# The down-projection of a ConvFFN written as seven block products, with operands made entry by entry

## The chip, the cores and the metric

The kernel runs on one core of one Trainium2 chip. The metric is the device time of one launch in microseconds (us). The measurement of this kernel before the change gave a median of 1247.1 us over three runs (1246.14 to 1247.32). One further execution was recorded by the hardware profiler; its own time is 1248.44 us, and its span, from the first to the last instruction, is 1246.7 us.

The engines are called PE (TensorE matmuls), PEld (its weight loads), DVE (VectorE), ACT (ScalarE), POOL (GpSimd) and SP (SyncE, which issues most DMA transfers).

## The reference

The kernel computes one layer of a streaming encoder for a prompt of 1024 tokens and eight sample sequences of 16 tokens (1152 tokens in all). A token mixer (spatial gating beside latent attention) is followed by a layer norm and a gated feed-forward network with a depthwise convolution of width 3:

```
up   = h @ w_up                       # (tokens, 1024) x (1024, 2*2816)
c    = causal_conv3(up) + b           # per channel, over the tokens
act  = silu(c[:, :2816]) * c[:, 2816:]
y    = act @ w_down                   # (tokens, 2816) x (2816, 1024)
out  = layer_norm(alpha * h + y)
```

The change concerns `act @ w_down` and what lies just ahead of it. Inputs and outputs are float32.

## The kernel before, in words

**Precision.** A float32 product is made of three matmuls on rounded parts. `split` writes the rounded value hi with ACT (`L60`) and the rest lo = x - hi with DVE (`L61`); `mm3` multiplies hi by hi, hi by lo and lo by hi (`L72` to `L74`), all summed in the same PSUM bank.

**Tiles.** There are 9 tiles of 128 tokens (8 of the prompt, one of the sample rows) and 22 blocks of 128 channels (`NF`). PSUM has eight banks of 512 columns, in four pools called A (3 banks), B (2), C (1) and D (2).

**Up-projection.** One iteration for each of the 22 channel blocks. Each makes seven block products (`product_mm`, `L932` to `L934`) instead of eight; ACT copies and DVE additions (`product`, `L1031` and `L1033`) put them into the output tiles `U`. An addition out of a bank frees it for the next product. The list `after(i)` is worked off between the products of the next iteration: the convolution (`conv`, ACT `L1038`, DVE `L1039` and `L1040`) and silu of one half, the convolution of the other half, and `gate` (DVE `L1052`), whose product of 1168 columns POOL writes to DRAM as `ad[i]` (`L1053`). The weights of the next iteration are added and split meanwhile (`L904`, `L907` and others, then `L60` and `L61`).

**Down-projection.** `load_down(i)` reads the activations of channel block i back from DRAM and its 128 x 1024 weights, and splits both into two tiles of a ring of 16. Blocks 0 to 3 are loaded during the last up-projection iteration. The 22 blocks are taken in five groups (`BLK`: 4, 4, 4, 4, 6). For each group, each token tile and each half of the 1024 output columns, `down_mm` sums the group's products in one PSUM bank, and DVE adds the bank to `y` in SBUF (`L1154`, `L1156`, in the last group `L1170` and `L1172`). So a block, once loaded, serves nine token tiles and two halves. In the first group `y` is first loaded and multiplied and shifted by the first layer norm's gain and bias (`L1148`, `L1149`). The last group is followed, tile by tile, by the second layer norm and the output. Its last token tile (the sample rows) computes its second half in two pieces of 256 columns, and the norm of that tile is what runs after the last matmul.

**Order.** A scheduler sets the order on each engine within the dependences; `pin` (`keep_in_program_order`) holds an instruction at the place where it is written. SP's DMA queue is worked off in order: a transfer that waits holds all that stand behind it.

## Time and profile before

| | |
|---|---|
| median of three runs | 1247.1 us (1246.14 to 1247.32) |
| profiled execution, its own time | 1248.44 us |
| its span | 1246.7 us |
| busy PE, PEld | 1227.5 us (98%), 1137.6 us |
| busy DVE, ACT, POOL | 844.6 us (68%), 533.1 us (43%), 97.7 us (8%) |
| last up-projection matmul starts | 972.34 us |
| last matmul of the down-projection starts | 1238.46 us |
| mean granted TensorE clock | 0.998 |

The profile gives, for each instruction, its line, its engine, the tile written and the tiles read, and its time; for idle time it names the event that ended it. Matmuls overlap on PE: the time shown for one is longer than its distance to the next, so its price is read from start to start. DMA issues show the time from issue to landing.

### The profile page before, as it was taken

Reading aid. Unit: us, or ns where it says so; the run is one execution under the profiler, and the core shown is the slowest. Engines: PE = TensorE matmul, PEld = TensorE weight load, DVE = VectorE, ACT = ScalarE, POOL = GpSimd, SP = SyncE. Lnnn points to the kernel's source line nnn. Section 1 sums busy time; section 2 is a strip of 40 time slices with the busy share of each in tenths; the row PEclk is TensorE's granted clock in tenths of the full one; section 3 lists DMA queues with packets and bytes.
Section 4 is the critical chain, followed back from the end, with each engine's and each line's share of the span. In section 5 each row is a group of like instructions: output and inputs, shape, how many; then the busy total and the mean of one; then the engine's idle time right before and its main releaser. Section 6 shows DMA issues by size and latency. Waiting matters only on the chain.

```text
span 1246.7 us, 19600 instructions
## 1 busy us (share of the span) xinstructions
PE 1227.5 (98%) x7737; PEld 1137.6 (91%) x7737; DVE 844.6 (68%) x1642; ACT 533.1 (43%) x1098; POOL 97.7 (8%) x229
## 2 busy tenths in 40 slices
...
DMA packets 35853, 116.47 MB, mean 93 GB/s; under 512 B 5120, under 2 KB 6272, under 8 KB 35760
## 3 DMA queue, kind: packets, MB, share of 16 engines
...
q8 instruction: 61, 1.00, 0.3%
q14 instruction: 32, 0.26, 0.1%
...
## 4 chain that ended last, share of the span: by engine, by line
PE 97%; ACT 1%; DVE 1%; DMA 1%; issue 0%; SPq 0%; ACTq 0%; DVEq 0%
PE A L934 8%; PE A L933 7%; PE A L932 7%; PE A L72 7%; PE A L73 7%; PE A L74 7%; PE D L72 7%; PE D L73 7%; PE D L74 7%; PE D L934 4%; PE D L933 4%; PE D L932 4%; PE B L72 2%; PE B L73 2%; PE B L74 2%; PE B L934 2%
## 5 line engine op out<-in xcount | busy, mean ns | idle before, releaser
L932 PE MATMUL A<-b,wu 128*128 128x288 f32 x704 | 207.6, 296 | 0.5 <-DVE U L1031 0.4
L933 PE MATMUL A<-b,wu 128*128 128x288 f32 x704 | 207.9, 296 | 0.0
L934 PE MATMUL A<-b,wu 128*128 128x288 f32 x704 | 206.0, 298 | 0.0
L932 PEld LDWEIGHTS A<-b,wu 128*128 128x128 f32 x704 | 132.4, 188 | 1.0 <-DVE U L1031 0.6
L933 PEld LDWEIGHTS A<-b,wu 128*128 128x128 f32 x704 | 132.8, 189 | 0.0
L934 PEld LDWEIGHTS A<-b,wu 128*128 128x128 f32 x704 | 131.1, 188 | 0.0
L934 PE MATMUL D<-b,wu 128*128 128x288 f32 x352 | 104.8, 298 | 0.0
L932 PE MATMUL D<-b,wu 128*128 128x288 f32 x352 | 104.1, 296 | 0.0
L933 PE MATMUL D<-b,wu 128*128 128x288 f32 x352 | 104.0, 295 | 0.0
L60 ACT ACTIVATE wu<-sc 128x512 fp32r<-128x512 f32 x66 | 41.8, 633 | 138.2 <-PE A L934 105.0
L60 ACT ACTIVATE b<-cbox 128x1024 fp32r<-128x1024 f32 (+1 forms) x40 | 25.6, 676 | 142.7 <-PE B L73 42.2
L61 DVE TENSOR_TENSOR wu<-sc,wu 128x512 fp32r<-128x512 f32 x66 | 46.2, 701 | 46.5 <-ACT wu L60 45.0
L1039 DVE SCALAR_TENSOR_TENSOR cbox<-U,raw,cbox 128x1168 f32<-128x1168 f32 x44 | 63.0, 1431 | 9.4 <-ACT cbox L1038 9.3
L933 PEld LDWEIGHTS D<-b,wu 128*128 128x128 f32 x352 | 66.4, 189 | 0.1
L932 PEld LDWEIGHTS D<-b,wu 128*128 128x128 f32 x352 | 66.1, 188 | 0.3 <-ACT b L60 0.3
L934 PEld LDWEIGHTS D<-b,wu 128*128 128x128 f32 x352 | 66.1, 188 | 0.0
L1040 DVE SCALAR_TENSOR_TENSOR cbox<-U,raw,cbox 128x1168 f32<-128x1168 f32 x44 | 63.0, 1431 | 0.8
L1038 ACT ACTIVATE cbox<-U,raw 128x1168 f32<-128x1168 f32 x44 | 60.0, 1363 | 7.3 <-DVE U L1031 7.1
L60 ACT ACTIVATE wu<-raw 128x512 fp32r<-128x512 f32 x66 | 41.6, 631 | 47.5 <-PE D L934 23.6
L1033 ACT ACTIVATE U<-A 128x288 f32<-128x288 f32 (+2 forms) x154 | 53.0, 368 | 17.5 <-PE A L934 17.5
L61 DVE TENSOR_TENSOR wu<-raw,wu 128x512 fp32r<-128x512 f32 x66 | 45.0, 685 | 14.5 <-ACT wu L60 14.5
L932 PE MATMUL B<-b,wu 128*128 128x288 f32 x176 | 52.1, 296 | 1.7 <-ACT hbox L855 1.7
...
## 6 DMA issues: line engine op xcount, KB each, us to landing
raw<-in_w_up SPq DMA_DIRECT2D x44, 512.0 KB, 3.2
ad<-cbox POOLq DMA_DIRECT2D x22, 584.0 KB, 3.1
cbox<-ad SPq DMA_DIRECT2D x22, 584.0 KB, 6.1
raw<-in_w_down SPq DMA_DIRECT2D x22, 512.0 KB, 5.7
xr<-in_xT SPq DMA_DIRECT2D x14, 512.0 KB, 4.1
y<-in_x SPq DMA_DIRECT2D x9, 512.0 KB, 3.6
nd<-y SPq DMA_DIRECT2D x9, 512.0 KB, 2.6
raw<-in_w_uv_in SPq DMA_DIRECT2D x8, 512.0 KB, 4.0
```

The costliest lines, as they stand in the source:

```text
L60: act.activation(hi, src, AF.Copy)
L61: dve.tensor_tensor(lo, src, f(hi), ALU.subtract)
L72: pe.matmul(out, lh, rh, start=first, stop=False)
L73: pe.matmul(out, lh, rl, start=False, stop=False)
L74: pe.matmul(out, ll, rh, start=False, stop=last)
L932: hold(pe.matmul(o_, lh, rh, start=first and k == 0, stop=False, skip_group_check=not first))
L933: hold(pe.matmul(o_, lh, rl, start=False, stop=False, skip_group_check=not first))
L934: hold(pe.matmul(o_, ll, rh, start=False, stop=k == 3, skip_group_check=not first))
L1033: act.activation(dst, src, AF.Copy)
L1038: act.activation(v, U[:, 2:n + 2], AF.Identity, bias=cw[:, fi, 3:4], scale=cw[:, fi, 2:3])
L1039: dve.scalar_tensor_tensor(v, U[:, 1:n + 1], cw[:, fi, 1:2], v, ALU.mult, ALU.add)
L1040: dve.scalar_tensor_tensor(v, U[:, 0:n], cw[:, fi, 0:1], v, ALU.mult, ALU.add)
```

## The change

The down-projection of the prompt's 1024 tokens is written as a product of 2 x 2 blocks: the tokens in two halves of 512 (`HT`), the channels in 11 pairs of blocks (`NPF`; the even block of a pair is one half, the odd one the other), and the output columns in two halves of 512. It uses seven block products with sums of activation blocks and sums of weight blocks, where eight products had been made. The sample rows are multiplied as before, as a ninth tile called `lone`.

The sums of activations are made in `after(i)` for odd i, when both blocks of a pair are there: four DVE operations of 512 columns (`L1069`, `L1070`, `L1074`, `L1075` of the new file) in the tiles of both gates. POOL then writes `ad[i-1]`, `an` (1024 columns) and `ax` (512 columns) to DRAM (`L1071`, `L1076`, `L1077`), beside `ad[i]` (`L1059`).

The operands are made by `produce()`, in the order of `ENTRY`: phases "2", "1", "65", "73" and "4", each over the 11 pairs. An entry reads its activations and weights (SP, `L1103` to `L1105` in the first two phases), makes sums of weights with DVE, and splits into two slots (one in phase "4") of a ring of 14. Phase "65" also writes a sum of weights to DRAM (`td`), which phase "4" reads. An entry of "2" or "1" serves four token tiles and the sample rows (18 matmuls), of "65" and "73" two products (24), of "4" one (12). `fill_ring` makes entries as far ahead as the ring has room. The entries 0 to 3 are made in the last up-projection iteration, in place of blocks 0 to 3.

Each product's bank is summed over all 11 pairs, so PSUM is added into `y` (`take`) at the end of a phase only, and the eight banks hold the running sums all the time. `y` is loaded and prepared (`first_y`) during the first two phases. At the end the second layer norm of the tiles follows phase "73" and runs beside phase "4", whose last token tile is computed in two pieces of 256 columns of one bank; the norm of tile 7, now the last one, follows.

```diff
+    an = [drp.tile([P, SEQ], F32, tag=f"an{i}", name=f"an{i}") for i in range(NPF)]
+    ax = [drp.tile([P, HT], F32, tag=f"ax{i}", name=f"ax{i}") for i in range(NPF)]
+    td = [drp.tile([P, HT], F32, tag=f"td{i}", name=f"td{i}") for i in range(NPF)]
...
         def gate():
             dve.tensor_tensor(cg[:, :n], ca[:, :n], cg[:, :n], ALU.mult)
-            pool.dma_start(ad[i], cg[:, :n])
+            if i % 2:
+                pool.dma_start(ad[i], cg[:, :n])
         l.append(gate)
-        return l
+        if i % 2 == 0:
+            even[:] = [ca, cg]
+            return l
+        spare, E = even
+        a00, a10, a01, a11 = E[:, :HT], E[:, HT:SEQ], cg[:, :HT], cg[:, HT:SEQ]
+        s5, s6, s3 = ca[:, :HT], ca[:, HT:SEQ], spare[:, :HT]
+
+        def sums_a():
+            dve.tensor_tensor(s5, a10, a11, ALU.add)
+            dve.tensor_tensor(a10, a00, a10, ALU.subtract)
+            pool.dma_start(ad[i - 1], E[:, :n])
+
+        def sums_b():
+            dve.tensor_tensor(s6, s5, a00, ALU.subtract)
+            dve.tensor_tensor(s3, a01, s6, ALU.subtract)
+            pool.dma_start(an[i // 2], ca[:, :SEQ])
+            pool.dma_start(ax[i // 2], s3)
+        return l + [sums_a, sums_b]
...
+    made, wslot, gone, raws = [], [0], [0], [raw_tile]
+    ENTRY = [(ph, p) for ph in ("2", "1", "65", "73", "4") for p in range(NPF)]
+    araw = [ctile[e] for e in (0, 3, 4)]
+
+    def slot():
+        wslot[0] += 1
+        return ring[(wslot[0] - 1) % len(ring)].rearrange("p c k i -> p (c k i)")
+
+    def both(ap, m):
+        return ap[:, :2 * m].rearrange("p (c m) -> p c m", c=2)
+
+    def produce():
+        ph, p = ENTRY[len(made)]
+        k = len(made)
+        ra = araw[k] if k < 3 else ctile[k % 3]
+        wr = raws[k % len(raws)]()
+        dn, up = a["w_down"][2 * p], a["w_down"][2 * p + 1]
+        if ph in ("2", "1"):
+            f_ = 2 * p + (ph == "2")
+            pin(sp.dma_start(ra[:, :HT], ad[f_][:, :HT]))
+            pin(sp.dma_start(ra[:, HT:HT + n - SEQ], ad[f_][:, SEQ:]))
+            pin(sp.dma_start(wr, a["w_down"][f_]))
+            sa, sb = slot(), slot()
+            wd, ac, lone = both(sa, D), both(sb, HT), both(sa[:, 2 * D:], P)
+            split(wd[:, 0], wd[:, 1], wr)
+            split(ac[:, 0], ac[:, 1], ra[:, :HT])
+            l4 = lone.rearrange("p c (b s) -> p c b s", b=NB)
+            split(l4[:, 0], l4[:, 1], ra[:, HT:HT + n - SEQ].rearrange("p (b s) -> p b s", b=NB)[:, :, 2:])
+            made.append((wd, ac, lone))
+            return
+        if ph == "4":
+            pin(sp.dma_start(ra[:, :HT], ad[2 * p + 1][:, HT:SEQ]))
+            pin(sp.dma_start(wr[:, :HT], td[p]))
+            sa = slot()
+            wd, ac = both(sa, HT), both(sa[:, D:], HT)
+            split(wd[:, 0], wd[:, 1], wr[:, :HT])
+            split(ac[:, 0], ac[:, 1], ra[:, :HT])
+            made.append((wd, ac, None))
+            return
+        if ph == "65":
+            pin(sp.dma_start(wr, dn))
+            wx = raws[(k + 1) % len(raws)]() if len(raws) > 1 else raw_tile()
+            pin(sp.dma_start(wx, up))
+            pin(sp.dma_start(ra[:, :SEQ], an[p]))
+            dve.tensor_tensor(wr[:, HT:], wr[:, HT:], wr[:, :HT], ALU.subtract)
+            dve.tensor_tensor(wr[:, :HT], wx[:, HT:], wr[:, HT:], ALU.subtract)
+        else:
+            pin(sp.dma_start(wr[:, :HT], dn[:, HT:]))
+            pin(sp.dma_start(wr[:, HT:], up[:, HT:]))
+            pin(sp.dma_start(ra[:, :HT], ad[2 * p][:, HT:SEQ]))
+            pin(sp.dma_start(ra[:, HT:SEQ], ax[p]))
+            dve.tensor_tensor(wr[:, :HT], wr[:, HT:], wr[:, :HT], ALU.subtract)
+        sa, sb = slot(), slot()
+        wd, ac = both(sa, D), both(sb, D)
         split(wd[:, 0], wd[:, 1], wr)
-        split(ac[:, 0, :SEQ], ac[:, 1, :SEQ], ra[:, :SEQ])
-        acs = ac[:, :, SEQ:].rearrange("p c (b s) -> p c b s", b=NB)
-        split(acs[:, 0], acs[:, 1], ra[:, SEQ:n].rearrange("p (b s) -> p b s", b=NB)[:, :, 2:])
-        ops[i] = (ac, wd)
+        split(ac[:, 0], ac[:, 1], ra[:, :SEQ])
+        if ph == "65":
+            dve.tensor_tensor(wx[:, :HT], wx[:, :HT], wr[:, :HT], ALU.subtract)
+            pool.dma_start(td[p], wx[:, :HT])
+        made.append((wd, ac, None))
...
-                    load_down(len(ops))
+                    produce()
...
-    BLK = [range(0, 4), range(4, 8), range(8, 12), range(12, 16), range(16, NF)]
-    dn, seq_d = [0], list("DBADBADBAC")
-
-    def down_mm(t, cols, blk):
-        b = bank(seq_d[dn[0] % len(seq_d)])
-        dn[0] += 1
-        m = cols.stop - cols.start
-        tok = slice(t * P, (t + 1) * P)
-        for j in blk:
-            ac, wd = ops[j]
-            mm3(b[:, :m], ac[:, 0, tok], ac[:, 1, tok], wd[:, 0, cols], wd[:, 1, cols], j == blk[0], j == blk[-1])
-        return b[:, :m]
-
...
+    raws.append(lambda: y2.tile([P, D], F32, tag="rw", name="rw", bufs=4))
+    sums = y2.tile([P, TT, 2], F32, tag="sums", name="sums")
+    ylate = {("2", 1 + 2 * t): t for t in range(4)}
+    ylate.update({("1", 1 + 2 * e): t for e, t in enumerate((8, 4, 5, 6, 7))})
+
+    def first_y(t):
         pin(sp.dma_start(y[t], nd[t]))
+        pin(dve.tensor_tensor(y[t], y[t], lg1, ALU.mult))
+        pin(dve.tensor_tensor(y[t], y[t], lb1, ALU.add))
+
+    def dmm(out, l, lc, r, rc, first, start, stop):
+        pe.matmul(out, l[:, 0, lc], r[:, 0, rc], start=start, stop=False, skip_group_check=not first)
+        pe.matmul(out, l[:, 0, lc], r[:, 1, rc], start=False, stop=False, skip_group_check=not first)
+        pe.matmul(out, l[:, 1, lc], r[:, 0, rc], start=False, stop=stop, skip_group_check=not first)
+
...
+    def take(t, c, b, fresh, acc=None):
+        yv = y[t][:, half[c]]
+        if acc is None and not fresh:
+            pin(dve.tensor_tensor(yv, yv, b, ALU.add))
+        else:
+            kw = {} if acc is None else {"accum_out": sums[:, t, c:c + 1]}
+            pin(dve.scalar_tensor_tensor(yv, yv, ALPHA if fresh else 1.0, b, ALU.mult, ALU.add, **kw))
+
+    def fill_ring(left):
+        while len(made) < len(ENTRY):
+            need = 1 if ENTRY[len(made)][0] == "4" else 2
+            if wslot[0] - gone[0] + need > len(ring) - left:
+                break
+            produce()
+
+    seg = [slice(e * P, (e + 1) * P) for e in range(2 * NT)]
+    full, P1 = slice(0, P), NPF - 1
+    Y = [bank(g) for g in "BBDD"]
+    L = [bank("A") for _ in range(2)]
+    X = Z = None
+    for k, (ph, p) in enumerate(ENTRY[:4 * NPF]):
+        fill_ring(2)
+        if (ph, p) in ylate:
+            first_y(ylate[ph, p])
+        wd, ac, lone = made[k]
+        if ph == "2":
+            for tp in range(NT):
+                dmm(Y[tp], ac, seg[tp], wd, half[0], True, p == 0, p == P1)
+        elif ph == "1":
+            if p == 0:
+                X = [bank(g) for g in "ACBB"]
+            for tp in range(NT):
+                dmm(X[tp], ac, seg[tp], wd, half[0], True, p == 0, p == P1)
+        else:
+            if p == 0 and ph == "65":
+                Z = [bank(g) for g in "DDAA"]
+            for tp in range(NT):
+                dmm(X[tp], ac, seg[tp + (NT if ph == "65" else 0)], wd, half[0], False, False, p == P1)
+            for tp in range(NT):
+                dmm(Z[tp], ac, seg[tp + (0 if ph == "65" else NT)], wd, half[1], ph == "65", p == 0 and ph == "65", p == P1)
+        if lone is not None:
+            for c in range(2):
+                dmm(L[c], lone, full, wd, half[c], True, ph == "2" and p == 0, ph == "1" and p == P1)
+        gone[0] += 2
+        if p == P1:
+            if ph == "2":
+                for tp in range(NT):
+                    take(tp, 0, Y[tp], True)
+            elif ph == "1":
+                for tp in range(NT):
+                    take(tp, 0, X[tp], False, True)
+                for c in range(2):
+                    take(NP, c, L[c], True, True)
+            elif ph == "65":
+                for tp in range(NT):
+                    take(tp, 1, X[tp], True)
+                for tp in range(NT):
+                    take(tp + NT, 1, Z[tp], True)
+            else:
+                for tp in range(NT):
+                    take(tp + NT, 1, X[tp], False, True)
+                for tp in range(NT):
+                    take(tp, 1, Z[tp], False, True)
+    fill_ring(0)
+    fin = made[4 * NPF:]
...
+    def end_mm(tp, cols):
+        for p, (wd, ac, _) in enumerate(fin):
+            dmm(X[tp][:, cols], ac, seg[tp], wd, cols, False, False, p == P1)
...
+    for tp, l in enumerate(((8, 0, 1), (2, 4), (3, 5), (6,))):
+        if tp < 3:
+            end_mm(tp, half[0])
+        else:
+            end_mm(tp, quart[0])
+            end_mm(tp, quart[1])
+        for e in l:
+            if e == 6:
+                for q in (2, 3):
+                    pin(dve.bn_stats(s6[:, q], yt[:, quart[q]]))
+            cur = norm_a(e, zs[zi % 3])
+            zi += 1
+            norm_b(prev)
+            prev = cur
+        if tp < 3:
+            take(tp + NT, 0, X[tp], True, True)
...
+    for e in (0, 1):
+        yv = yt[:, quart[e]]
+        pin(dve.scalar_tensor_tensor(yv, yv, ALPHA, X[3][:, quart[e]], ALU.mult, ALU.add))
+        pin(dve.bn_stats(s6[:, e], yv))
...
```

**DVE in an odd iteration of the up-projection.** The rows follow the last convolution. `U` is an output tile of the up-projection, `cbox` the storage of the gates, `wu`, `sc` and `raw` belong to the next weights. Before:

```order
L1031 TENSOR_TENSOR U<-U,B 128x288
L61 TENSOR_TENSOR wu<-raw,wu 128x512
L1052 TENSOR_TENSOR cbox<-cbox 128x1168
L61 TENSOR_TENSOR wu<-raw,wu 128x512
L61 TENSOR_TENSOR wu<-sc,wu 128x512
L907 TENSOR_TENSOR sc<-sc,raw 128x512
L1031 TENSOR_TENSOR U<-U,D 128x288
```

Now:

```order
L1035 TENSOR_TENSOR U<-U,B 128x288
L61 TENSOR_TENSOR wu<-raw,wu 128x512
L1057 TENSOR_TENSOR cbox<-cbox 128x1168
L61 TENSOR_TENSOR wu<-raw,wu 128x512
L1069 TENSOR_TENSOR cbox<-cbox 128x512
L1070 TENSOR_TENSOR cbox<-cbox 128x512
L1074 TENSOR_TENSOR cbox<-cbox 128x512
L61 TENSOR_TENSOR wu<-sc,wu 128x512
L1075 TENSOR_TENSOR cbox<-cbox 128x512
L911 TENSOR_TENSOR sc<-sc,raw 128x512
L1035 TENSOR_TENSOR U<-U,D 128x288
```

The four sums stand between the gate and the addition out of bank D.

**SP between the up- and the down-projection.** `ad_44..` are the activations in DRAM, `cbox` the raw activations in SBUF, `nd` the saved residual. Before, around blocks 2 to 4:

```order
L1066 DMA cbox<-ad_4456 128x1168
L1134 DMA raw<-in_ln_b 128x1024
L1139 DMA y_10742<-nd_4444 128x1024
L1139 DMA y_10743<-nd_4445 128x1024
L1147 DMA y_10744<-nd_4446 128x1024
L1066 DMA cbox<-ad_4457 128x1168
L1068 DMA raw<-in_w_down 128x1024
```

Now, entries 3, 4 and the start of 5:

```order
L1103 DMA cbox<-ad_4460 128x512
L1104 DMA cbox<-ad_4460 128x144
L1105 DMA raw<-in_w_down 128x1024
L1189 DMA raw<-in_ln_b 128x1024
L1272 DMA raw<-in_ln_g 128x1024
L1103 DMA cbox<-ad_4462 128x512
L1104 DMA cbox<-ad_4462 128x144
L1105 DMA raw<-in_w_down 128x1024
L1103 DMA cbox<-ad_4464 128x512
```

The read of `ad_4462` is entry 4's. Its target is the tile from which the last `ax` is written; it and all behind it stand after that write.

**PE at the end of phase "1".** The first entries of phase "65" follow; the bank letters are pools, `b_...` ring slots. Before, at the same distance behind the up-projection, a bank was filled by a group of blocks and left:

```order
L72 MATMUL D<-b_5450,b_5147 128x512
L73 MATMUL D<-b_5450,b_5147 128x512
L74 MATMUL D<-b_5450,b_5147 128x512
L72 MATMUL D<-b_5453,b_5248 128x512
L73 MATMUL D<-b_5453,b_5248 128x512
L74 MATMUL D<-b_5453,b_5248 128x512
```

Now the products in bank D of four entries stand first, those in bank A, which the phase before has filled, behind them (the first and the last of the four entries, and the first rows on A):

```order
L1202 MATMUL D<-b_5281,b_5486 128x512
L1203 MATMUL D<-b_5281,b_5486 128x512
L1204 MATMUL D<-b_5281,b_5486 128x512
...
L1202 MATMUL D<-b_5469,b_5498 128x512 x2
L1203 MATMUL D<-b_5469,b_5498 128x512
L1204 MATMUL D<-b_5469,b_5498 128x512
...
L1202 MATMUL A<-b_5281,b_5486 128x512
L1203 MATMUL A<-b_5281,b_5486 128x512
L1204 MATMUL A<-b_5281,b_5486 128x512
```

24 matmuls into bank D stand between the last product of phase "1" and the first that needs an emptied bank of that phase.

More of the change, by code (lines that the diff above doesn't have):

```diff
@@ L1042, in trunk @@
     U_ = {}
+    even = []
     def after(i):
@@ L1131, in trunk @@
-    half = [slice(0, 512), slice(512, D)]
-    y = []
+    NT = NP // 2
+    half = [slice(0, HT), slice(HT, D)]
     lb1 = raw_w()
     pin(sp.dma_start(lb1, a["ln1_b"].partition_broadcast(P)))
-    for t in range(TT):
-        y.append(y2.tile([P, D], F32, tag=f"y{t}", name=f"y{t}") if t < 7 else ctile[t - 4][:, :D])
-    ring += [y2.tile([P, 2, 4, NH], F32R, tag=f"rg{e}", name="rg") for e in range(2)]
-    for t in range(2):
-        pin(sp.dma_start(y[t], nd[t]))
-    nxt = list(range(4, NF))
@@ L1141, in trunk @@
-    for bi, blk in enumerate(BLK[:-1]):
-        for t in range(TT):
-            if nxt and t % 2 == 1:
-                load_down(nxt.pop(0))
-            if bi == 0:
-                if t + 2 < TT:
-                    pin(sp.dma_start(y[t + 2], nd[t + 2]))
-                pin(dve.tensor_tensor(y[t], y[t], lg1, ALU.mult))
-                pin(dve.tensor_tensor(y[t], y[t], lb1, ALU.add))
-            for g in range(2):
-                b = down_mm(t, half[g], blk)
-                yv = y[t][:, half[g]]
-                if bi == 0:
-                    dve.scalar_tensor_tensor(yv, yv, ALPHA, b, ALU.mult, ALU.add)
-                else:
-                    dve.tensor_tensor(yv, yv, b, ALU.add)
@@ L1157, in trunk @@
-    while nxt:
-        load_down(nxt.pop(0))
+    y = [y2.tile([P, D], F32, tag=f"y{t}", name=f"y{t}") if t < 7 else ctile[t - 4][:, :D] for t in range(TT)]
+    raws.append(lambda: y2.tile([P, D], F32, tag="rw", name="rw", bufs=4))
[3 more added lines that the diff above has]
+    def first_y(t):
+        pin(sp.dma_start(y[t], nd[t]))
+        pin(dve.tensor_tensor(y[t], y[t], lg1, ALU.mult))
+        pin(dve.tensor_tensor(y[t], y[t], lb1, ALU.add))
```

62 lines of the change are left out of this document (19 added, 43 removed).

## The prediction

> **What bounds the kernel now.** I read the page's busy times and its chain first, then windows around the down-projection, then the matmuls one by one.
>
> ```profile
> PE 1227.5 (98%) x7737; PEld 1137.6 (91%) x7737; DVE 844.6 (68%) x1642; ACT 533.1 (43%) x1098; POOL 97.7 (8%) x229
> PE 97%; ACT 1%; DVE 1%; DMA 1%; issue 0%; SPq 0%; ACTq 0%; DVEq 0%
> ```
>
> TensorE is busy for 98% of the span and makes up 97% of the chain that ends last. A matmul that is taken away shortens the run by its own time, as long as the matmuls that stay are still fed. The windows below cut the end of the run: last up-projection block, first two groups of the down-projection, the rest of it, and what follows the last matmul. Columns: window, its length, busy time of PE, PEld, DVE, ACT and POOL, granted clock, DMA share, GB/s.
>
> ```profile
> 960.00:969.00 9.00, 9.00 (x54) 8.15 (x53) 4.98 (x11) 3.32 (x4) 0.94 (x3) 1.00 0.25 102
> 969.00:1040.00 71.00, 70.68 (x320) 58.41 (x319) 62.50 (x72) 21.44 (x28) 0.53 (x1) 1.00 0.74 277
> 1040.00:1238.80 198.80, 198.74 (x889) 164.11 (x887) 88.67 (x173) 43.12 (x62) 16.00 (x7) 1.00 0.17 61
> 1238.80:1246.70 7.90, 0.00 (x0) 0.00 (x0) 4.58 (x12) 0.20 (x1) 0.00 (x0) 0.74 0.21 83
> ```
>
> PE has 0.4 us of gaps in 270, although DVE is nearly full (62.50 of 71.00) in the second window: a block loaded before is used by nine token tiles, so there is slack everywhere. 7.9 us run without matmuls at the end.
>
> **The change, part by part.** *Matmuls removed.* Before: 22 blocks x 9 tiles x 2 halves x 3 = 1188 products of 512 columns, 18 of them cut into 36 of 256. Now: 7 products x 11 pairs x 4 tiles x 3 = 924, plus 22 x 2 x 3 = 132 for the sample rows, together 1056, 33 of them cut into 66. Their prices, start to start:
>
> ```profile
> 1230.19 0.39 PE L72 MATMUL A<-b,b 128*128 128x512 f32 x1
> 1234.05 0.39 PE L74 MATMUL A<-b,b 128*128 128x512 f32 x1
> 1234.27 0.28 PE L72 MATMUL C<-b,b 128*128 128x256 f32 x1
> 1238.46 0.28 PE L74 MATMUL D<-b,b 128*128 128x256 f32 x1
> ```
>
> The first two rows are the first and the last of 18 matmuls: (1234.05 - 1230.19) / 17 = 0.227 us. The others are the first and the last of 36: 4.19 / 35 = 0.120 us. Before: 1170 x 0.227 + 36 x 0.120 = 269.9 us. Now: 1023 x 0.227 + 66 x 0.120 = 240.1 us. **Saved: 29.8 us.**
>
> *The hand-over from the up- to the down-projection.* This term is the largest against the gain. Before, the four blocks loaded by then give 216 matmuls. Now the first four entries give 4 x 18 = 72, and 13 of these stand ahead of the last up-projection product; behind it stand 59 x 0.227 = 13.4 us of work. Entry 4 then needs a chain which begins with that same product, because its raw activations go into the tile that held the last third sum (`spare`), which must first be written to DRAM (`ax`). I call the start of the last up-projection matmul U. The chain up to the write of the last activations can be read before the change:
>
> ```profile
> 972.34 0.30 PE L934 MATMUL A<-b,wu 128*128 128x288 f32 x1
> 973.48 1.36 ACT L1038 ACTIVATE cbox<-U,raw 128x1168 f32<-128x1168 f32 x1
> 974.88 1.44 DVE L1039 SCALAR_TENSOR_TENSOR cbox<-U,raw,cbox 128x1168 f32<-128x1168 f32 x1 [3.30 <-ACT cbox L1038]
> 976.35 1.44 DVE L1040 SCALAR_TENSOR_TENSOR cbox<-U,raw,cbox 128x1168 f32<-128x1168 f32 x1
> 977.82 1.38 DVE L1052 TENSOR_TENSOR cbox<-cbox 128x1168 f32<-128x1168 f32 x1
> 979.60 0.53 POOL L1053 DMA_DIRECT2D ad<-cbox  x1 [11.14 <-DVE cbox L1052]
> ...
> 995.24 0.68 DVE L1154 SCALAR_TENSOR_TENSOR y<-y,B 128x512 f32<-128x512 f32 x1
> 995.84 0.68 DVE L1154 SCALAR_TENSOR_TENSOR y<-y,A 128x512 f32<-128x512 f32 x1
> ...
> ad<-cbox POOLq DMA_DIRECT2D x22, 584.0 KB, 3.1
> raw<-in_w_up SPq DMA_DIRECT2D x44, 512.0 KB, 3.2
> raw<-in_w_down SPq DMA_DIRECT2D x22, 512.0 KB, 5.7
> 985.00:990.00 5.00, 5.00 (x24) 4.14 (x23) 4.97 (x7) 1.06 (x1) 0.00 (x0) 1.00 1.02 420
> L60 ACT ACTIVATE b<-raw 128x1024 fp32r<-128x1024 f32 x20 | 21.1, 1056 | 4.8 <-DMA raw<-in_w_down 4.8
> ```
>
> The gate ends at 977.82 + 1.38 = 979.20, U + 6.9. Four sums of 512 columns follow; a 512-column operation takes DVE 0.60 us start to start (995.24 to 995.84), with dependences at most 0.68, so 2.4 to 2.7: U + 9.5. POOL issues three writes before and then the fourth, 0.5 us each; the first three mostly pass while DVE still sums: fourth issued at U + 10.0 to 10.5. It landed 3.1 us later for 584 KB alone; here 256 KB stands behind 584 + 584 + 512 KB, 1.7 MB, of which at 420 GB/s 4.1 us are needed, partly gone by then. So it lands at U + 13.1 to 15; I take 14. Only then can SP issue entry 4's activations, sample rows and weights (842 KB; nothing behind them on SP's queue passes): 3.2 us by the nearest unhurried 512 KB, 5.7 by the queue-bound one. 842 KB at 420 GB/s alone are 2.0; I take 3.8, near the lower, because the queue is empty then. The ACT copy of the weights adds 1.06 us (21.1 / 20). Entry 4 is ready at U + 18.9 against U + 13.4: **stall 5.5 us**, bounds 13.1 + 3.2 + 1.06 - 13.4 = 4.0 and 15 + 5.7 + 1.06 - 13.4 = 8.4. Below 4.0 only if the writes land quicker than any row here; I allow 2.8.
>
> *The clock after that stall.* What an idle TensorE does to its clock is seen at the two ends of the run:
>
> ```profile
> 1241.70:1242.20 0.50, 0.00 (x0) 0.00 (x0) 0.50 (x2) 0.00 (x0) 0.00 (x0) 1.00 0.00 0
> 1242.20:1242.70 0.50, 0.00 (x0) 0.00 (x0) 0.50 (x1) 0.00 (x0) 0.00 (x0) 0.91 0.00 0
> 1242.70:1243.20 0.50, 0.00 (x0) 0.00 (x0) 0.47 (x2) 0.00 (x0) 0.00 (x0) 0.50 0.28 111
> 9.52 0.69 PE L72 MATMUL A<-w,xs 128*128 128x384 f32 x1 [2.37 <-ACT w L60]
> 13.01 0.47 PE L72 MATMUL D<-w,xs 128*128 128x320 f32 x1
> 13.27 0.47 PE L73 MATMUL D<-w,xs 128*128 128x320 f32 x1
> 15.16 0.31 PE L72 MATMUL D<-w,xs 128*128 128x320 f32 x1
> 15.30 0.30 PE L73 MATMUL D<-w,xs 128*128 128x320 f32 x1
> ```
>
> The granted clock (third column from the right) goes from 1.00 to 0.50 at about 1242.6, 3.9 us after the last matmul ended (1238.46 + 0.28). At the start 320-column matmuls are 0.26 us apart at 13.01 and 0.14 at 15.16; work that began at 9.52 ran at half rate until about 13.6, some 4.1 us, half of them lost. A stall over 3.9 us therefore costs another **2.0 us**; bounds 0 and 2.1. I take it, since 5.5 is over 3.9.
>
> The Trainium skill ("TensorE: Matmul & The Clock Gate", Part 1) puts this down to a free-running activity window of about 3.4 us: one wholly idle window halves the clock, a busy one restores it. Its rule would let a 5.5 us stall miss a whole window in some placements, so by it the sum is 1226 or 1224. The one drop seen here, after 3.9 us, agrees with such a window but shows only one placement.
>
> *Just-in-time operands.* From entry 4 on an operand serves one entry, 18 x 0.227 = 4.1 us of PE (24 x 0.227 = 5.4 in the two double phases). DVE's price is read here:
>
> ```profile
> 993.91 0.28 DVE L61 TENSOR_TENSOR b<-cbox,b 128x128 fp32r<-128x128 f32 x1
> 994.11 1.22 DVE L1148 TENSOR_TENSOR y<-y,cbox 128x1024 f32<-128x1024 f32 x1
> ```
>
> 1024 columns take 995.24 - 994.11 = 1.13 us, 512 take 0.60, 128 take 0.20. An entry of phases "2" and "1" costs DVE 1.13 + 0.60 + 0.20 = 1.9, every second one 2.3 more for a y tile: 3.1 on average under 4.1. "65" costs 2 x 1.13 + 3 x 0.60 = 4.1 under 5.4, "73" 2.9 under 5.4, "4" 1.2 under 2.7. DMA brings 1.84 MB in and out per "65" entry, 337 GB/s, below the 420 seen. All hidden behind PE, so 0, but the end of phase "1" is tight: from entry 4 DVE has 18 x 1.9 + 8 y tiles x 2.3 + five "65" entries made ahead x 4.1 + four additions x 0.6 = 75.5 us before the additions that free the banks, PE 18 x 4.1 = 73.8. The 2 us by which DVE is late are covered by the bank-D products of four entries, 24 x 0.227 = 5.4 us, which PE takes first (the listing of PE). With that cover gone, 2 us. For the three phase changes I book 0.5 us.
>
> *PSUM additions.* Before, 5 groups x 9 tiles x 2 halves = 90 bank sums (and one more for a cut half) were added into y, now 31; the 60 fewer (0.60 us of DVE each) were beside PE: 0.
>
> *Tail.* After the last matmul:
>
> ```profile
> 1238.78 0.42 DVE L1170 TENSOR_TENSOR cbox<-cbox,D 128x256 f32<-128x256 f32 x1
> 1239.24 0.43 DVE L1210 BATCH_NORM_STATS2 s<-cbox 128x6 f32<-128x256 f32 x1
> ```
>
> An addition and its statistics take 0.42 + 0.43. Before, one quarter remained; now two, which share a bank: **+0.9 us**.
>
> *Sums in the up-projection.* Odd iterations get the four sums (2.6 us) behind the gate on DVE, ahead of additions that free PSUM banks:
>
> ```profile
> 885.58 1.37 DVE L1052 TENSOR_TENSOR cbox<-cbox 128x1168 f32<-128x1168 f32 x1
> 890.80 0.69 DVE L61 TENSOR_TENSOR wu<-sc,wu 128x512 fp32r<-128x512 f32 x1 [2.51 <-ACT wu L60]
> 892.14 0.45 DVE L1031 TENSOR_TENSOR U<-U,D 128x288 f32<-128x288 f32 x1
> 893.41 0.46 DVE L1031 TENSOR_TENSOR U<-U,A 128x288 f32<-128x288 f32 x1 [0.82 <-PE A L934]
> ...
> PE A L932 <- DVE U L1031: 0.4, 1, 0.4
> ```
>
> Between gate and additions DVE idles 2.51 us, and 0.82 behind the first: 3.3 over 2.6, so 0. In the whole up-projection PE waited for such an addition once, 0.4 us (last row: waited for in total, times, longest). With that cover gone: 11 x 2.6 = 28.6 us.
>
> *Sum* against the profiled execution: 1248.44 - 29.8 + 5.5 + 2.0 + 0.9 + 0.5 = 1227.5. It stands 1.3 above the median of the runs shown (1247.1), so **1226 us**.
>
> **The rivals.**
> - *Hand-over hidden.* The write of the third sum lands early and entry 4 is there in time, or the stall stays under 3.9 us and the clock up: 1226.2 - 7.5 = 1218.7 to 1226.2 - 2.0 - 1.5 = 1222.7. For it: writes are small beside 420 GB/s. Against: the chain's DVE part alone takes 9.5 of the 13.4 us. Also in this group: a 5.5 us stall with the clock kept, 1224.2.
> - *Operands late throughout.* DVE is 75% full in the first two phases and each entry passes load, ACT, DVE; 22 entries 0.3 to 0.5 us late are 7 to 11 us: 1233 to 1237. For it: DVE's 62.50 of 71.00 at a similar mix, and the ring is empty after the stall. Against: six entries of lookahead.
> - *Slower: the sums push the PSUM releases.* If DVE's idle 2.51 us cannot be used (the ACT copy waited for lands behind the sums), each odd iteration stalls PE by up to 2.6 us: 1226.2 + 28.6 = 1255. It decides from 20.9 / 11 = 1.9 us per odd iteration. Against: the idle times above.
> - *It does not do what it says*: the products remain eight or are split finer. The listing has 1023 + 66 matmuls; I give this none.
>
> **How the numbers follow.** Chances: forecast with stall and half clock 0.45; hand-over hidden or clock kept 0.25; operands late 0.20; slower 0.05; a mixture between 1238 and 1247 0.05. The range 1217 to 1238 holds the first three but for a little. Over 0.2%, about 2.5 us, is what a measurement tells from no change: faster 0.92, same 0.02, slower 0.06.
>
> **What would show it.** In the new profile: PE at 0.227 us per 512 columns with 1089 matmuls; one wait of 4 to 8 us some 13 us after the last up-projection matmul, for an operand copied by ACT, its DMA behind the `ax` write; a window of granted clock 0.50 behind it; no such wait in later phases; no new wait of the up-projection's matmuls for additions that free banks; last addition to end 0.9 us longer. I am wrong if PE waits in every entry, or if the up-projection grows.

## The result and the profile after

The changed kernel takes 1231.03 us (median of four runs, 1230.36 to 1231.93) against 1246.62 us before on the same chip: a ratio of 0.9871, 95% interval 0.9858 to 0.9883. The forecast was 1226, the range 1217 to 1238. The profiled execution took 1231.93 us, its span is 1230.2 us: 16.5 us less than before, where the working had 20.9.

First the busy times and the chain by engine, from the page of the changed kernel, and two rows of what PE waited for (in total, times, longest).

```profile
PE 1198.2 (97%) x7620; PEld 1115.4 (91%) x7620; DVE 919.2 (75%) x1737; ACT 580.7 (47%) x1164; POOL 117.8 (10%) x262
PE 91%; DVE 3%; ACT 2%; issue 2%; DMA 1%; SPq 0%; POOL 0%; ACTq 0%; POOLq 0%; DVEq 0%
```

```profile
PE B L1202 <- ACT b L60: 6.9, 1, 6.9
PE A L936 <- DVE U L1035: 0.4, 1, 0.4
```

PE has 117 matmuls less, as counted. DVE, ACT and DMA now hold 6% of the chain; before, PE held 97% of it. There is one new wait, of 6.9 us in this list (7.1 us of time lost, as worked out below), and the wait of the up-projection for an emptied bank is 0.4 us once, as before. The windows show where the time lies (columns as in the prediction):

```profile
968.20:990.00 21.80, 14.87 (x71) 12.21 (x69) 8.08 (x11) 5.17 (x8) 2.16 (x4) 0.93 0.60 213
990.00:1000.00 10.00, 10.00 (x37) 8.15 (x38) 9.32 (x13) 6.86 (x12) 0.00 (x0) 0.82 1.03 404
1000.00:1060.00 60.00, 60.00 (x267) 49.69 (x266) 59.63 (x79) 31.83 (x48) 1.64 (x3) 1.00 0.95 362
1060.00:1120.00 60.00, 60.00 (x266) 49.73 (x265) 51.97 (x66) 25.48 (x26) 4.33 (x8) 1.00 0.95 350
1120.00:1180.00 60.00, 60.00 (x266) 49.69 (x266) 36.70 (x48) 24.18 (x34) 0.00 (x0) 1.00 0.52 167
1180.00:1215.30 35.30, 35.30 (x188) 30.47 (x186) 30.65 (x72) 18.47 (x29) 15.32 (x6) 1.00 0.19 77
1215.30:1230.20 14.90, 0.09 (x1) 0.00 (x0) 10.19 (x27) 1.65 (x4) 2.34 (x1) 0.62 0.35 137
```

From 1000 to 1215 PE has no gap at all, though DVE is busy for 59.63 of 60 us in the first of these windows. All that was lost lies in two places: 7 us without work and a lower clock between 968 and 1000, and 14.9 us behind the last matmul, where there had been 7.9.

**The hand-over.** Timeline of the changed kernel, then its chain over the same stretch (start, length, what):

```profile
969.25 0.30 PE L938 MATMUL A<-b,wu 128*128 128x288 f32 x1
...
977.89 0.69 DVE L1075 TENSOR_TENSOR cbox<-cbox 128x512 f32<-128x512 f32 x1
...
979.10 0.55 POOL L1077 DMA_DIRECT2D ax<-cbox  x1
...
982.55 0.39 PE L1204 MATMUL A<-b 128*128 128x512 f32 x1
989.87 1.22 PE L1202 MATMUL B<-b,b 128*128 128x512 f32 x2 [6.93 <-ACT b L60]
...
994.02 0.39 PE L1203 MATMUL D<-b,b 128*128 128x512 f32 x1
```

```profile
979.10 3.98 DMA ax<-cbox
...
983.98 4.76 DMA raw<-in_w_down
...
988.76 1.06 ACT b L60
```

What SP waited for just before entry 4's first load:

```profile
SPq L1103 <- DMA ax<-cbox: 8.3, 1, 8.3
```

With U = 969.25, the last sum ends at U + 9.3, the fourth write is issued at U + 9.9 and lands at U + 13.8, the weights of entry 4 land at U + 19.5, and PE goes on at U + 20.6. Its work had ended at 982.55 + 0.23 = U + 13.5. The stall is 7.1 us.

The granted clock, us by us around its fall and its return (third column from the right):

```profile
985.00:986.00 1.00, 0.00 (x0) 0.00 (x0) 0.00 (x0) 0.35 (x1) 0.00 (x0) 1.00 0.95 189
986.00:987.00 1.00, 0.00 (x0) 0.00 (x0) 0.69 (x2) 0.48 (x2) 0.00 (x0) 0.92 0.95 301
987.00:988.00 1.00, 0.00 (x0) 0.00 (x0) 0.21 (x2) 0.00 (x0) 0.00 (x0) 0.50 0.83 290
...
993.00:994.00 1.00, 1.00 (x4) 0.82 (x3) 1.00 (x2) 0.69 (x2) 0.00 (x0) 0.67 1.00 406
994.00:995.00 1.00, 1.00 (x6) 0.82 (x5) 0.94 (x3) 0.55 (x1) 0.00 (x0) 1.00 1.06 402
```

It falls at about 986.8, 4 us after PE ran dry, and is back at about 993.7, 3.8 us after PE went on. The ten matmuls behind the stall take 994.02 - 989.87 = 4.15 us instead of 10 x 0.227 = 2.27: 1.9 us.

**The end.** Selected rows of DVE, POOL and PE around the last matmul, and the groups of two of DVE's instructions (count, busy, mean ns), in the changed kernel:

```profile
1203.73 3.13 POOL L1283 TENSOR_TENSOR y<-cbox,raw 128x1024 f32<-128x1024 f32 x1 [1.47 <-ACT cbox L1282]
1205.13 1.74 DVE L100 SCALAR_TENSOR_TENSOR rt<-ry,rh 128x1 f32<-128x1 f32 x1 [0.22 <-ACT ry L90]
1211.91 2.41 POOL L1283 TENSOR_TENSOR y<-cbox,raw 128x1024 f32<-128x1024 f32 x1 [1.47 <-ACT cbox L1282]
1212.15 3.27 DVE L1290 SCALAR_TENSOR_TENSOR cbox<-y,sm,raw 128x1024 f32<-128x1024 f32 x1
1215.11 0.28 PE L1204 MATMUL B<-b 128*128 128x256 f32 x1
1217.62 2.34 POOL L1283 TENSOR_TENSOR y<-cbox,raw 128x1024 f32<-128x1024 f32 x1 [3.29 <-ACT cbox L1282]
1217.67 2.30 DVE L100 SCALAR_TENSOR_TENSOR rt<-ry,rh 128x1 f32<-128x1 f32 x1 [0.99 <-ACT ry L90]
1221.53 0.41 DVE L1329 SCALAR_TENSOR_TENSOR cbox<-cbox,B 128x256 f32<-128x256 f32 x1
```

```profile
L100 DVE SCALAR_TENSOR_TENSOR rt<-ry,rh 128x1 f32<-128x1 f32 x45 | 17.5, 388 | 6.9 <-ACT ry L90 6.0
L1290 DVE SCALAR_TENSOR_TENSOR cbox<-y,sm,raw 128x1024 f32<-128x1024 f32 x7 | 11.0, 1567 | 0.6
```

The last matmul starts at 1215.11, but DVE adds its bank only at 1221.53: DVE is 6 us behind with the norms of the other tiles. An instruction on one element per partition takes 1.74 and 2.30 us, and ends each time when a POOL addition ends (1203.73 + 3.13 = 1206.86 and 1205.13 + 1.74 = 1206.87; 1219.96 and 1219.97). The 3.27 us of `L1290`, which elsewhere takes 1.28, end 1.10 us after POOL's addition (1214.32). POOL touches none of the tiles of `L100`, and DVE's list of waits from 1180 on has no wait for POOL, so this is no wait for data. Before, the same 45 instructions of `L100`, and the seven of `L1290` (there `L1192`), were not held:

```profile
L100 DVE SCALAR_TENSOR_TENSOR rt<-ry,rh 128x1 f32<-128x1 f32 x45 | 9.8, 219 | 3.6 <-ACT ry L90 2.7
L1192 DVE SCALAR_TENSOR_TENSOR cbox<-y,sm,raw 128x1024 f32<-128x1024 f32 x7 | 9.0, 1293 | 0.6
```

That kernel has the same seven additions on POOL, of 2.0 to 2.4 us each. They stood some 8 us apart, mostly where DVE waited for PE.

The account in spans: matmuls -29.8; stall +7.1; clock +1.9; from the last matmul's start to the end 15.1 instead of 8.2, +6.9; together -13.9 of the measured -16.5. Of the other 2.6, 1.9 lie in the kernel before, and the working did not have them: from 972.47 to 1234.27 its 1145 matmuls of 512 columns took 0.2286 us each instead of 0.227, with one gap of 0.5 us in it (the last section has more). The last up-projection matmul starts 3.1 us earlier instead of the 2.7 that twelve matmuls make.

### The profile page after: what moved, and what is told of

Same layout as the page of the kernel before. It is cut to its first block, busy times and chain, and to the rows that moved or that the text cites. A ratio compares the mean times of both kernels' runs of the same rounds, so it can differ in the third digit from the quotient of the medians.

```text
span 1230.2 us, 19933 instructions
## 1 busy us (share of the span) xinstructions
PE 1198.2 (97%) x7620; PEld 1115.4 (91%) x7620; DVE 919.2 (75%) x1737; ACT 580.7 (47%) x1164; POOL 117.8 (10%) x262
## 4 chain that ended last, share of the span: by engine, by line
PE 91%; DVE 3%; ACT 2%; issue 2%; DMA 1%; SPq 0%; POOL 0%; ACTq 0%; POOLq 0%; DVEq 0%
PE A L938 8%; PE A L937 7%; PE A L936 7%; PE A L72 5%; PE A L73 5%; PE A L74 5%; PE D L72 4%; PE D L73 4%; PE D L74 4%; PE D L938 4%; PE D L937 4%; PE D L936 4%; PE A L1202 2%; PE A L1203 2%; PE A L1204 2%
## 5 line engine op out<-in xcount | busy, mean ns | idle before, releaser
L60 ACT ACTIVATE b<-cbox 128x512 fp32r<-128x512 f32 (+2 forms) x77 | 48.6, 654 | 72.0 <-DMA cbox<-ad 18.7
L61 DVE TENSOR_TENSOR b<-cbox,b 128x512 fp32r<-128x512 f32 (+2 forms) x77 | 53.9, 723 | 31.8 <-ACT b L60 25.8
L1037 ACT ACTIVATE U<-A 128x288 f32<-128x288 f32 (+2 forms) x154 | 53.3, 369 | 20.7 <-PE A L938 20.6
```

What stands on the lines that cost most here:

```text
L60: act.activation(hi, src, AF.Copy)
L61: dve.tensor_tensor(lo, src, f(hi), ALU.subtract)
L1037: act.activation(dst, src, AF.Copy)
```

## The experiments

The theories after the two traces. **A**: the stall comes from entry 4's tile, which waits for the last `ax` write, and the half clock from the stall. **C**: the late end comes from DVE instructions that stand still while POOL adds (phase "4"). Their rivals are **B** (the transfers are late in any case) and **D** (DVE has simply too much work in phase 4). Ratios are against the kernel before, run beside each; the changed kernel itself stands at 0.9871, so 0.0008 is one microsecond. U lies between 968.5 and 969.5 in these executions, with nearly the same work up to there, so a difference of two spans carries up to 1 us from ahead of U.

**1. A tile of its own for entry 4.**

```diff
-        ra = araw[k] if k < 3 else ctile[k % 3]
+        ra = araw[k] if k < 3 else raws[1]() if k == 4 else ctile[k % 3]
```

> Entry 4's raw activations go into a tile of their own instead of the one whose last third sum must first be written to DRAM; nothing else changes. Theory A (the wait of 6.9 us between entries 3 and 4 comes from that write, and the half clock behind it from the wait): entry 4 is ready before the 59 matmuls in front of it are done, both losses go, 7.1 + 1.9 = 9.0 us, time about 1222. Rival B (the transfers behind the writes are late in any case): the wait moves to entry 5, whose tile waits for the write of the even block; then 2 to 5 us of the 7.1 stay, the clock keeps up, time 1224 to 1227.

Measured: 1224.53 us, ratio 0.9817 (0.9802 to 0.9832); span 1223.0, 7.2 us less than with the change alone. PE's row for the hand-over:

```profile
PE B L1202 <- ACT b L60: 1.3, 1, 1.3
```

The stall of 7.1 and the half clock are gone (the clock is 1.00 in every window from 980 to 996), as A has it. 1.3 us of waiting came up one entry later, as B has it, though smaller: SP waits 6.3 us there for the write of the even block. Why the time does not fall by those 1.3 us when this wait goes too, run 6 shows.

**2. Matmuls that keep PE busy in the stall.** 28 extra matmuls, whose result nothing reads, stand between entries 3 and 4; the result is complete.

```diff
         wd, ac, lone = made[k]
+        if k == 4:
+            idle = bank("C")
+            for e in range(28):
+                pin(pe.matmul(idle, made[3][1][:, 0, seg[0]], made[3][0][:, 0, half[0]], start=e == 0, stop=e == 27))
```

> 28 extra matmuls of 512 columns (6.35 us, on operands that are there, into a bank that nothing reads) between entries 3 and 4; the wait for entry 4 stays. Theory A (the 10 slow matmuls behind the wait are slow because the clock fell to half): the granted clock stays 1.00, entry 4's matmuls start 0.227 us apart at once, and 1.9 us are saved, time about 1229. Rival (they are slow because operands come late): no gain, time 1231, the matmuls behind the wait 0.43 us apart as before.

Measured: 1229.24 us, ratio 0.9856 (0.9839 to 0.9872); span 1227.5, 2.7 us less.

```profile
982.00:990.00 8.00, 7.97 (x36) 6.28 (x35) 2.31 (x4) 2.72 (x5) 0.00 (x0) 1.00 0.77 246
990.00:994.00 4.00, 4.00 (x20) 3.29 (x19) 2.86 (x6) 2.85 (x4) 0.00 (x0) 1.00 1.03 401
```

The clock stays at 1.00 and the four microseconds from 990 hold 20 matmuls instead of 10. So the ten slow ones were slow for the clock. The saving in spans is 0.8 above the 1.9 expected, but 0.7 of that lies ahead of the extra matmuls: U is 968.55 in this execution instead of 969.25. From U to the end the saving is 2.0.

**3. No addition on POOL.** The second norm's bias is left out for seven of nine tiles.

```diff
-        act.activation(z, z, AF.Copy, scale=rs)
-        pool.tensor_tensor(y[t], z, lb2, ALU.add)
+        act.activation(y[t], z, AF.Copy, scale=rs)
```

> The addition of the second norm's bias by POOL is left out for seven of the nine token tiles (ACT writes the scaled rows into y, from where they are sent out). Theory C (in phase 4 DVE instructions with two SBUF inputs stand still until a POOL addition ends, 1 to 2 us each, and the norms so run 6 us behind PE): the 128x1 instructions of L100 take 0.22 us again, DVE is done with the norms when the last matmul ends, from its start to the end 9 us instead of 15, time about 1225. Rival D (DVE has simply more work than phase 4 lasts, or waits for ACT): the end comes less than 2 us earlier, 1229 or more.

Measured: 1224.94 us, ratio 0.9821 (0.9806 to 0.9835); span 1223.5. Groups of this kernel, then its last matmul and the addition of its bank:

```profile
L100 DVE SCALAR_TENSOR_TENSOR rt<-ry,rh 128x1 f32<-128x1 f32 x45 | 9.8, 218 | 7.0 <-ACT ry L90 6.1
L1289 DVE SCALAR_TENSOR_TENSOR cbox<-y,sm,raw 128x1024 f32<-128x1024 f32 x7 | 9.0, 1285 | 0.2
```

```profile
1214.56 0.28 PE L1204 MATMUL B<-b 128*128 128x256 f32 x1
1214.87 0.42 DVE L1328 SCALAR_TENSOR_TENSOR cbox<-cbox,B 128x256 f32<-128x256 f32 x1 [0.99 <-PE B L1204]
```

`L100` is back at 218 ns, DVE waits for PE at the end (0.99 us) instead of adding the last bank 6 us late, and the end comes 6.7 us earlier; from the last matmul's start it takes 8.9 us instead of 15.1. C stands: DVE has the same instructions as in the changed kernel, so D would have left it behind PE.

**4. The bias added by DVE instead.**

```diff
-        act.activation(z, z, AF.Copy, scale=rs)
-        pool.tensor_tensor(y[t], z, lb2, ALU.add)
+        pin(dve.scalar_tensor_tensor(y[t], z, rs, lb2, ALU.mult, ALU.add))
```

> The same seven tiles: one DVE instruction scales and adds the bias (1.2 us), in place of ACT's scaling and POOL's addition. No POOL addition runs beside DVE. Theory C: seven waits of 1.0 to 2.1 us (9.6 together) go, 7 x 1.2 = 8.4 come, but the ACT copy and its waits leave the chain as well: the end 1 to 3 us earlier, 1228 to 1230. Rival D (DVE's work is the bound): 8.4 us more DVE work lengthen the end, 1233 to 1239.

Measured: 1228.8 us, ratio 0.985 (0.9836 to 0.9865); span 1226.9, 3.3 us less than with the change alone. DVE does seven instructions of 1.28 us more and is done earlier all the same. In the changed kernel POOL's additions held DVE for (17.5 - 9.8) + (11.0 - 9.0) = 9.7 us, the groups of `L100` and `L1290` against those of run 3; seven instructions of 1.28 us are 9.0, and ACT's scaling leaves the chain with its waits. From the last matmul's start to the end it still takes 12.2 us. DVE adds the last bank at 1218.29, 3.3 us after PE is done: with this work added, D's limit does hold.

**5. The sample tile's norm in phase "73".** The norm's functions, and the loads of its gain and bias, move ahead of phase "2" for it (not shown).

```diff
...
+        if ph == "73" and p == 3:
+            early = norm_a(NP, y[NP])
+        if ph == "73" and p == 5:
+            norm_b(early)
...
-    for tp, l in enumerate(((8, 0, 1), (2, 4), (3, 5), (6,))):
+    for tp, l in enumerate(((0, 1), (2, 4), (3, 5), (6,))):
```

> The second norm of the sample tile, whose sums are complete after phase 1, runs in phase 73 instead of at the start of phase 4; nothing is left out, POOL still adds the bias. Theory C/D together (the end is set by DVE's queue in phase 4, of which a norm takes some 4 us): the last addition out of PSUM and the end come about 4 us earlier, time 1227 to 1228. Rival (the chain at the end is ACT's and POOL's, not DVE's amount of work): under 1 us earlier, 1231.

Measured: 1229.81 us, ratio 0.9856 (0.9841 to 0.987); span 1227.8, 2.4 us less. That lies between the two expectations: one norm less moves the end by 2.4 of its 4 us. The POOL additions still hold DVE (`L100` takes 306 ns in the mean).

**6. Tiles of their own for entries 4 and 5.** As run 1, with `k in (4, 5)`.

> As the run with a tile of its own for entry 4, now for entry 5 too. Theory A (the 1.3 us that were left there come from entry 5's wait for the write of the even block): no wait is left at the hand-over, 1.3 us less than with one tile of its own, time 1223. Rival (what was left is the transfers' own time, 3 to 5 us with three entries' loads at once): the wait stays 1 us or more, time 1224 to 1225.

Measured: 1224.67 us, ratio 0.9817 (0.98 to 0.9833); span 1222.5. Theory A was right on the wait and wrong on the time, the rival the other way round. The wait at the hand-over is gone entirely, and the time is that of run 1, since another wait has come:

```profile
PE A L1202 <- DVE y L1212: 1.7, 1, 1.7
```

It stands at 1062.9, at the end of phase "1": PE waits for DVE to take the sums out of the banks. First the start of that addition and PE's first matmul into bank A in the changed kernel, then the addition in this run, and what SP waited for here:

```profile
1066.73 0.68 DVE L1212 SCALAR_TENSOR_TENSOR y<-y,A 128x512 f32<-128x512 f32 x1
1070.64 0.39 PE L1202 MATMUL A<-b,b 128*128 128x512 f32 x1
```

```profile
1062.13 0.68 DVE L1212 SCALAR_TENSOR_TENSOR y<-y,A 128x512 f32<-128x512 f32 x1
```

```profile
SPq L1103 <- DMA ax<-cbox: 11.6, 1, 11.6
```

PE would have come to bank A at 1061.0, 9.6 us earlier than in the changed kernel; DVE came only 4.6 us earlier. SP still waits for the `ax` write here, 11.6 us, now with the load of a later entry. PE has entries made before to work on meanwhile, but DVE is idle for 5.9 of the 10 us from 985 on, waiting for those loads. The wait has passed from PE to DVE. The prediction had worked out 2 us of lateness under a cover of 5.4. Here the cover is used up and 1.7 us of waiting stand behind it, so the lateness is 7.1.

**7. More work for DVE in phases "2" and "1".** One unused subtraction of 512 columns in each of the entries 4 to 21.

```diff
+            if k >= 4:
+                dve.tensor_tensor(wr[:, :HT], wr[:, :HT], wr[:, HT:], ALU.subtract)
             made.append((wd, ac, lone))
```

> One DVE subtraction of 512 columns more (0.60 us, its result is not used) in each of the entries 4 to 21, 10.8 us in all, in the phases 2 and 1 where DVE is 99% busy. Theory E (DVE is at the edge there, with the 5.4 us of bank-D products as its only cover beyond 2 us of lateness): PE waits 6 to 8 us at the end of phase 1, time 1237 to 1239. Rival F (the ring's entries made ahead leave more cover, since DVE was busy with later entries): PE waits under 2 us, time 1231 to 1233.

Measured: 1243.45 us, ratio 0.9966 (0.9953 to 0.9979); span 1241.7, 11.5 us more than with the change alone for 10.8 us of work. Rows of PE's waits, and windows of the stretch where most of them lie:

```profile
PE D L1205 <- DVE b L61: 3.8, 2, 2.2
PE D L1204 <- ACT b L60: 2.1, 2, 1.5
PE A L1204 <- DVE y L1214: 0.9, 1, 0.9
```

```profile
1068.00:1070.00 2.00, 0.47 (x2) 0.43 (x3) 2.00 (x4) 0.00 (x0) 0.54 (x1) 1.00 0.91 307
1070.00:1072.00 2.00, 1.37 (x6) 0.74 (x4) 2.00 (x4) 1.06 (x1) 0.00 (x0) 0.79 0.85 281
1072.00:1074.00 2.00, 0.58 (x2) 0.00 (x0) 2.00 (x3) 0.00 (x0) 0.54 (x1) 0.50 0.95 352
1074.00:1076.00 2.00, 1.26 (x3) 1.08 (x4) 2.00 (x3) 0.00 (x0) 0.00 (x0) 0.50 0.99 371
```

PE waits 3.8 + 2.1 + 0.9 = 6.8 us, the 6 to 8 of theory E. What E did not have is the clock: it fell to 0.50 over these waits, none of which is longer than 2.2 us, and 18 matmuls started at half rate before it rose again at about 1084.8. They took 0.43 us each instead of 0.227, some 3.7 us; the last microsecond is not accounted for. DVE is at the edge in these phases even with the stall's help.

**8. Three parts together** (runs 4, 5 and 6).

> Entries 4 and 5 in tiles of their own, the sample tile's norm in phase 73, and the bias added by DVE instead of POOL; the whole result is computed. The parts that the theories name add up: 7.1 + 1.9 us at the hand-over, and a tail of 9 us instead of 15, together 15 us, time 1216 to 1217. Rival (DVE, with 1.2 us per tile more, still ends behind PE): 2 us of the tail stay, 1218 to 1219.

Measured: 1221.05 us, ratio 0.9785 (0.9771 to 0.98). Neither expectation: the tail was right, but 1.6 us of waiting were back at the hand-over and 1.7 us at the end of phase "1". The load of the second norm's gain stands ahead of entry 4's loads here, as in run 5, and goes out at 974.24 only; entry 4's begin at 974.67 instead of 967.12 in run 6. From the last matmul's start to the end it takes 9.5 us, near the 9 expected.

**9. The residual of tiles 4 to 7 prepared in phase "65"** (with run 6).

```diff
-    ylate.update({("1", 1 + 2 * e): t for e, t in enumerate((8, 4, 5, 6, 7))})
+    ylate["1", 1] = 8
+    ylate.update({("65", 1 + 2 * e): t for e, t in enumerate((4, 5, 6, 7))})
```

> As the run with tiles of their own for entries 4 and 5, and the residual of tiles 4 to 7 is loaded and prepared (2.3 us of DVE each) in phase 65, where it is first needed at the end, instead of in phase 1. Theory G (the 1.7 us wait at the end of phase 1 comes from DVE being behind, and with 9.1 us less work it is not): that wait goes, PE runs without a gap from the up-projection to the last matmul, 1.7 us less, time 1223. Rival (the additions out of the banks are late for another reason, or DVE falls behind in phase 65 instead): the wait stays or moves, 1224.5 or more.

Measured: 1223.06 us, ratio 0.9799 (0.9784 to 0.9815); span 1221.5, 1.0 less than run 6. The wait is gone from the list, and PE has no wait in the down-projection. Theory G holds. The medians lie 1.6 us apart and the intervals of the two ratios overlap, so the gain in time is not shown by itself; the missing wait is. From U to the end this execution is 1.9 us shorter than run 6's.

**10. All parts**, with the second norm's gain and bias loaded in phase "73".

> All parts together: own tiles for entries 4 and 5, the sample tile's norm in phase 73, the bias added by DVE, the residual of tiles 4 to 7 prepared in phase 65, and the second norm's gain and bias loaded in phase 73 instead of at the hand-over. Theories A, C and G: both waits that were left in the run with three of these parts (1.6 us at the hand-over, 1.7 us at the end of phase 1) go, 3.3 us less than its 1221.05, time 1217.5 to 1218. Rival (each wait removed lets another queue be late, as at the end of phase 1): 1220 to 1221.

Measured: 1216.96 us (1215.93 to 1217.77), ratio 0.9748 (0.9734 to 0.9762). PE from the hand-over to the last matmul, and what is left behind it:

```profile
970.00:1206.80 236.80, 236.66 (x1076) 197.12 (x1074) 200.10 (x302) 106.18 (x147) 8.13 (x15) 1.00 0.74 273
1206.80:1216.00 9.20, 0.00 (x0) 0.00 (x0) 5.81 (x15) 0.20 (x1) 0.00 (x0) 0.61 0.33 126
```

This kernel computes the whole result and beats both: by spans 14.3 us below the changed kernel and 30.8 below the kernel before. What the removed matmuls are worth arrives nearly whole: PE has 0.14 us of gaps, and the end, from the last matmul's start at 1206.38, takes 9.5 us instead of 8.2, 1.3 us more, near the +0.9 that the prediction had booked.

## Why the prediction was right, and which step failed

- **Matmuls, 29.8 us.** Right. PE ran at 0.227 us per 512 columns from 1000 to 1207 without a gap, 1089 matmuls in all.
- **Stall, 5.5 us (4.0 to 8.4).** The mechanism was right in each link, the size 7.1. Sum done at U + 9.3 (9.5 predicted), write landed at U + 13.8 (14). The link that was too small is the load of entry 4: 3.8 us were taken "because the queue is empty then", and the trace has 5.7 from the landed write to the landed weights (983.08 to 988.74), the upper bound. The queue was empty, yet nothing moved in the first microsecond, and from 984.08 to 988.74 the engines moved 258 GB/s, some 1.2 MB, where entry 4 needs 0.86 MB (840 KB): SP had issued the loads of entries 5 and 6 right behind, and they had a part of it. How much each of the three costs was not tried.
- **Clock, 2.0 us.** Right: 1.9, and run 2 shows that the clock is the cause. The rivals in which the clock is kept up fell with it.
- **Tail, 0.9 us.** The step "before, one quarter remained; now two, which share a bank: +0.9 us" failed: the end came 6.9 us later than before, measured from the last matmul. The working read the tail from the instructions behind the last matmul alone, and took it that DVE would be there when PE ends, as before. But the change also gathers eight second norms beside phase "4", whose matmuls last 30.5 us (1184.88 to 1215.39), where before each had the 8 us in which PE made the next tile. The costing of the change went past that part, and past what POOL does to DVE in it. Runs 3 and 4 show the cause: without POOL's additions the tail is 6.2 us shorter (8.9), and with the same additions on DVE 2.9 us shorter (12.2), though DVE then has 9.0 us more to do.
- **Just-in-time operands, 0 and 0.5 us.** Right for the changed kernel, where nothing waits. The first bank of phase "1" was free at 1067.4, 2.2 us behind that phase's last matmul (1065.2), where 2 had been worked out. In part that is luck: nine y tiles, not eight, follow entry 4 (2.3 us more for DVE), and the half clock held PE back by 1.9. Run 6 shows what the sum left out, that DVE itself can be kept waiting at the hand-over: 1.7 us of waiting appeared, with the bank-D cover still in place. Run 7 shows that little slack was left.
- **Sums in the up-projection, 0.** Right: the last up-projection matmul starts no later than twelve removed matmuls make it, and PE's wait for an emptied bank is 0.4 us, as before.
- **The rivals.** "Hand-over hidden" was wrong, "operands late throughout" did not occur but was near, "slower" did not occur. What moved the time from 1226 to 1231 was in none of them.
- **What was luck.** In spans the terms came out 7.0 us worse than booked (tail +6.0, stall +1.6, clock -0.1, phase changes -0.5), and the 2.6 us that the working did not have came to its help: the miss is 4.4. That 1231 lies inside the range owes something to this, and to room that the range had for late operands, which did not come.

The Trainium skill ("SBUF — State Buffer", "SBUF: two separate sides") has the rule that was missing here: GpSimd and DVE share a pair of ports that is locked for a whole instruction, and a DVE instruction with two SBUF inputs stands against a GpSimd one that reads SBUF. The trace agrees: the held instructions, `L100` and `L1290`, read two SBUF tiles, and each held `L100` ends within 0.02 us of POOL's addition. An instruction with one such input, `L87` at 1208.50, took its usual 0.15 us while POOL added. With this rule beside the code, 7 additions of 2.1 to 3.1 us on POOL in the new phase "4" could have been counted against DVE in advance.
